# One core, two layers: the first norm's factor and offset folded into the second modulation's rows in two partitions

## The chip, the cores and the metric

The kernel runs on one core of a Trainium2 chip. Its time is device time in microseconds (us), from the start of the program to its end. The kernel before took 1130.2 us, the median of three runs (1126.81, 1130.2 and 1132.19).

The core has five engines with instruction queues of their own: TensorE (PE in the profile; PEld is its weight loads), VectorE (DVE), ScalarE (ACT), GpSimd (POOL) and SyncE (SP), which here only issues transfers (DMAs). Each engine works its queue in order, and waits on semaphores for the others.

## The reference, cut to what matters

One step of a network of two layers for 128 context tokens and 256 latent tokens, with 1024 columns. Each layer has a token mixer and a mixture of experts (MoE). Both are modulated by six rows that come from a conditioning vector, one set for the latent tokens and one for the context tokens:

```python
m = silu(cvec) @ w_ada + b_ada                     # 6 x 1024 columns
sh1, sc1, g1, sh2, sc2, g2 = split(m, 6)
mix = token_mixer(x * (1 + sc1) + sh1)
x = layer_norm(ALPHA * x + g1 * mix, ln1_g, ln1_b)
y = hier_moe(x * (1 + sc2) + sh2)
x = layer_norm(ALPHA * x + g2 * y, ln2_g, ln2_b)
```

What the MoE reads is therefore, with n the normed row before its factor and offset, `(n * ln1_g + ln1_b) * (1 + sc2) + sh2`. This equals `n * G + B`, with `G = ln1_g * (1 + sc2)` and `B = ln1_b * (1 + sc2) + sh2`. G and B are two rows of 1024 numbers for each of the two token sets. Both kernels work with G and B; they differ in where these are formed.

## The kernel before, in words

**Tiles.** The 384 tokens are three tiles of 128 partitions (tile 0 the context, tiles 1 and 2 the latents). Weights stream from HBM through a ring of buffers `w_raw` of 1 MB; ScalarE and VectorE split each piece into two parts (`wr`, lines 102 and 110), and TensorE multiplies it as three products (lines 97 to 99 and 488 to 490).

**The modulation rows.** The generator `ada(l, g)` works out a third of the six rows of layer l: g = 0 gives sh1 and sc1, g = 1 gives g1 and sh2, g = 2 gives sc2 and g2. TensorE's result lies in four stretches of 512 columns, and stretch t in the two partitions 32t and 32t + 1 (latent and context row). That is the tile `adasb`. For g = 1 and 2 the bias row is added to it (line 243), for g = 2 the first two stretches get + 1 (line 245), and four small transfers on GpSimd's queue write it into a table in DRAM, `m_d` (line 247). The generator runs beside the mixer: the loop `mixer` calls it again every few weight pieces, and the instructions between two `yield`s come in one go.

**After the mixer.** `open_ln1` frees the mixer's tiles and loads rows from `m_d`, each spread over all 128 partitions: g1 (line 891), sc2 and sh2, and the norm's factor `lg` and offset `lb`. On GpSimd it then forms G in the place of sc2 and B in the place of sh2: three passes over 128 x 1024 for each token set, six for a layer (lines 911 to 913, product `rtmp` first). Meanwhile TensorE runs the output projection (lines 488 to 490), column block by column block. For each tile of a block VectorE multiplies the result by g1 (line 946, which reads PSUM), adds ALPHA x (line 949, both inputs in SBUF) and takes the norm's statistics (line 952); TensorE transposes the sum for the router (line 963) and multiplies it (line 970). The last block stands in `last_col`: there VectorE applies G (line 999) and B (line 1002) to the whole row, and the routing follows, then the MoE.

**What sets the order.** In the mixer a scheduler places the instructions on each engine: it simulates the program with a cost model and takes what is ready first. The first 50 us (`start`, the table STEPS) and `last_col` stand in an order written by hand. SyncE's transfers stand in one queue. In the built program each of them waits, besides for its buffer, for an earlier transfer: there are eight semaphores taken in turn (DMAHW0 to 7), and a transfer waits until the one before it on its semaphore has landed.

Of the kernel before, what the change touches and what calls it, by code (L numbers as in the profile page):

```python
# [20 lines left out]
D = 1024  # L21
# [58 lines left out]
class Kern:  # L80
# [130 lines left out]
    def ada(self, l, g):  # L211

        nc, a = self.nc, self.a
        ps = self.bank("ms")
        for kp in range(4):
            for k in range(2):
                w = self.get(("a", l, g, kp, k))
                for t in range(4):
                    nc.tensor.matmul(ps[32 * t:32 * t + 32, :], self.cT[:, 2 * kp + k, :],  # L219
                                     w[:, t * 512:t * 512 + 512],  # L220
                                     start=(kp == 0 and k == 0), stop=(kp == 3 and k == 1))
                self.done()
            yield
        sb = self.mix.tile([128, 512], F32, tag="tmp", name="adasb", bufs=3)
        self.act(sb, ps, AF.Copy)
        yield
        p2 = self.bank("ms")
        for j in range(4):
            nc.tensor.transpose(p2[:, j * 128:(j + 1) * 128], sb[:, j * 128:(j + 1) * 128], self.ident)
        mT = self.mT[l]  # L230
        nc.vector.tensor_tensor(
            mT[:, g * 16:(g + 1) * 16, :].rearrange("p (t j) s -> p j t s", j=4),
            p2.rearrange("p (j t r) -> p j t r", j=4, t=4)[:, :, :, 0:2],
            self.bT[:, l, g * 16:(g + 1) * 16].rearrange("p (t j) -> p j t", j=4)
            .unsqueeze(3).to_broadcast([128, 4, 4, 2]),
            op=ALU.add)
        if g != 1:
            j = 8 if g == 0 else 32
            nc.vector.tensor_scalar(mT[:, j:j + 8, :], mT[:, j:j + 8, :], 1.0, None, op0=ALU.add)
        if g > 0:  # L240
            br = self.mix.tile([128, 512], F32, tag="tmp", name="adabr", bufs=3)
            nc.sync.dma_start(br, a["badar"][l * 2 + g - 1])
            nc.vector.tensor_tensor(sb, sb, br, op=ALU.add)
            if g == 2:
                nc.vector.tensor_scalar(sb[0:64, :], sb[0:64, :], 1.0, None, op0=ALU.add)
            for t in range(4):
                nc.gpsimd.dma_start(self.m_d[l][g - 1, :, t * 512:(t + 1) * 512], sb[32 * t:32 * t + 2, :])
        yield
# [627 lines left out]
    def open_ln1(self, l):  # L876
# [12 lines left out]
        def load(name, src, pool):  # L889
            t = pool.tile([128, 1024], F32, tag=name if pool is self.lp else "row", name=name, bufs=1 if pool is self.lp else 2)  # L890
            nc.sync.dma_start(t, src.to_broadcast([128, 1024]))
            rows[name] = t
            return t
# [6 lines left out]
        src = a["x"] if l == 0 else self.x_d  # L900
        nc.sync.dma_start(xs[0], src[0:256, :].rearrange("(i p) c -> p i c", p=128))
        nc.sync.dma_start(xs[1][:, 0], src[256:T, :])
        g = load("lg", a["ln"][l * 4:l * 4 + 1, :], self.mo)
        b = load("lb", a["ln"][l * 4 + 1:l * 4 + 2, :], self.mo)
        for s in range(2):
            load(f"sc2{s}", md[1, s:s + 1, 0:1024], self.lp)
            load(f"sh2{s}", md[0, s:s + 1, 1024:2048], self.lp)
        for s in range(2):
            sc, sh = rows[f"sc2{s}"], rows[f"sh2{s}"]
            t = self.lp.tile([128, D], F32, tag="t", name="rtmp", bufs=2)  # L910
            nc.gpsimd.tensor_tensor(t, sc, b, op=ALU.mult)  # L911
            nc.gpsimd.tensor_tensor(sh, sh, t, op=ALU.add)
            nc.gpsimd.tensor_tensor(sc, sc, g, op=ALU.mult)
        self.st1 = self.sm.tile([128, NT, 4, 6], F32, tag="st1", name="st1", bufs=1)

    def route_consts(self, l):
# [1056 lines left out]
```

## Time and profile before

| what | value |
|---|---|
| runs | 1126.81, 1130.2, 1132.19 us; median 1130.2 |
| profiled execution: own time, span of the trace | 1127.33 us, 1125.6 us |
| TensorE busy, share of the span | 1011.2 us, 90% |
| VectorE busy | 810.7 us, 72% |
| ScalarE busy | 417.4 us, 37% |
| GpSimd busy | 269.7 us, 24% |
| mean granted clock of TensorE | 0.959 of full speed |

A busy share is a mean over stages with different limits. Layer 0's mixer ends near 372 us and its MoE near 555 us; layer 1's mixer runs from some 590 to 918 us, and its MoE to the end. In the listings a time is us from the span's start, and the bracket at a row's end is the engine's idle time before that instruction and what ended it.

### The profile page before, as it was taken

How to read it: one execution, taken by the hardware profiler on the slowest of the kernel's cores; microseconds unless marked ns; L12 is line 12 of the kernel's file. 1: busy time of each engine (PE TensorE's matmuls, PEld its weight loads, DVE VectorE, ACT ScalarE, POOL GpSimd, SP SyncE). 2: the span in 40 equal slices, each digit the busy share in tenths (PEclk: the TensorE clock that was granted, in tenths of full speed). 3: DMA queues.
4: the chain of work that ended last, by engine and by line, in shares of the span. 5: the costliest groups of instructions: out<-in, count | busy, mean ns of one | idle time of the engine just before them, and what ended most of it. 6: DMA issues, size and time to landing. Idle time of an engine off the chain costs nothing. (4 is left out here: it accounts for less than half of the span.)

```text
span 1125.6 us, 20806 instructions
## 1 busy us (share of the span) xinstructions
PE 1011.2 (90%) x8182; PEld 840.7 (75%) x8182; DVE 810.7 (72%) x1530; ACT 417.4 (37%) x753; POOL 269.7 (24%) x232
## 2 busy tenths in 40 slices
PE   7999999999999999776689998999999999778673
PEld 5898978877999988433259897788999998754322
DVE  4399999965446986762569999997834587777437
ACT  4324254434333324341163443445532341434221
POOL 0001431221100510333244043114111025013335
PEclk9999999999999989897989999999999999989888
DMA  9967668447436667799585756773223666689955
GB/s 358 412 241 257 266 217 294 178 163 270 151 112 246 259 262 293 303 420 403 219 315 201 280 217 233 251 290 127 110 94 132 224 244 229 227 317 416 419 204 194
DMA packets 55101, 282.75 MB, mean 251 GB/s; under 512 B 8060, under 2 KB 12284, under 8 KB 27857
## 3 DMA queue, kind: packets, MB, share of 16 engines
q1 hardware_dynamic: 49632, 270.01, 63.1%
q0 software_dynamic: 5360, 11.29, 2.7%
q8 instruction: 69, 1.13, 0.4%
q14 instruction: 40, 0.32, 0.1%
HBM read 262.13 MB, written 24.71 MB: 255 GB/s over the span
## 5 line engine op out<-in xcount | busy, mean ns | idle before, releaser
L97 PE MATMUL ps_mm<-hThi,wr 128*128 128x384 f32 x672 | 229.9, 343 | 4.4 <-ACT hThi L102 2.3
L110 DVE TENSOR_TENSOR wr<-w_raw,wr 128x1024 fp32r<-128x1024 f32 x124 | 162.2, 1309 | 92.4 <-ACT wr L102 92.3
L98 PE MATMUL ps_mm<-hTlo,wr 128*128 128x384 f32 x672 | 228.0, 340 | 0.6 <-DVE hTlo L441 0.4
L99 PE MATMUL ps_mm<-hThi,wr 128*128 128x384 f32 x672 | 227.5, 339 | 0.6 <-DVE wr L110 0.6
L102 ACT ACTIVATE wr<-w_raw 128x1024 fp32r<-128x1024 f32 x140 | 147.5, 1055 | 68.1 <-PE ps_mm L99 37.8
L505 DVE SCALAR_TENSOR_TENSOR cacc<-pad,par,cacc 128x399 f32<-128x399 f32 x240 | 169.2, 705 | 4.2
L97 PEld LDWEIGHTS ps_mm<-hThi,wr 128*128 128x128 f32 x672 | 127.1, 189 | 18.2 <-issue 4.0
L98 PEld LDWEIGHTS ps_mm<-hTlo,wr 128*128 128x128 f32 x672 | 127.1, 189 | 6.3 <-DVE hTlo L441 2.5
L99 PEld LDWEIGHTS ps_mm<-hThi,wr 128*128 128x128 f32 x672 | 127.2, 189 | 2.5 <-DVE wr L110 0.9
L110 POOL TENSOR_TENSOR wr<-w_raw,wr 128x1024 fp32r<-128x1024 f32 x10 | 24.5, 2447 | 201.6 <-ACT wr L102 201.2
L1458 POOL DMA_INDIRECT y_d<-ys,dst x28 | 28.4, 1016 | 172.3 <-DVE hv L1400 73.3
L1446 PE MATMUL ps_sc<-w,hidT 128*32 128x512 f32 x256 | 43.1, 766 | 28.6 <-ACT ys L102 21.9
L1415 PE MATMUL ps_mm<-hv,win 128*32 128x128 f32 x1024 | 46.4, 277 | 9.2 <-DVE hv L1400 7.8
L1400 DVE COPY hv<-w_raw 128x512 f32 x60 | 41.9, 737 | 16.6 <-PE ps_mm L1415 10.8
L1415 PEld LDWEIGHTS ps_mm<-hv,win 128*32 128x32 f32 x1024 | 35.8, 112 | 22.7 <-DVE hv L1400 12.0
L1409 PE MATMUL ps_mm<-w_raw,win 128*32 128x256 f32 x640 | 47.8, 391 | 3.5 <-ACT win L102 3.5
L219 PE MATMUL ps_ms<-w_raw,cT 128*32 128x512 f32 x320 | 48.7, 612 | 1.4 <-DMA w_raw<-in_wada 1.4
L102 ACT ACTIVATE gate<-ps_mm 128x384 f32<-128x384 f32 x40 | 19.6, 490 | 81.6 <-PE ps_mm L99 80.5
L1446 PEld LDWEIGHTS ps_sc<-w,hidT 128*32 128x32 f32 x256 | 8.2, 123 | 45.8 <-ACT ys L102 32.9
L911 POOL TENSOR_TENSOR rtmp<-sc,lb 128x1024 f32<-128x1024 f32 x4 | 9.8, 2478 | 121.8 <-DMA lb<-in_ln 121.8
L842 POOL TENSOR_TENSOR merged<-merged,gate 128x384 f32<-128x384 f32 x16 | 18.1, 1135 | 87.0 <-DVE gate L841 87.0
L102 ACT ACTIVATE win<-xT 128x256 f32 x64 | 21.5, 409 | 37.6 <-PE ps_mm L1409 30.2
(505 smaller groups left out, 2355.7 us busy)
## 6 DMA issues: line engine op xcount, KB each, us to landing
w_raw<-in_wst SPq DMA_DIRECT2D x68, 1024.0 KB, 6.4
w_raw<-in_wada SPq DMA_DIRECT2D x48, 1024.0 KB, 5.4
w_raw<-in_w SPq DMA_DIRECT2D x40, 1024.0 KB, 10.7
w<-in_w SPq DMA_DIRECT2D x32, 1024.0 KB, 12.3
w_x<-in_w SPq DMA_DIRECT2D x24, 1024.0 KB, 11.8
bias<-in_bias SPq DMA_DIRECT2D x8, 768.0 KB, 7.6
y_d<-zero SPq DMA_DIRECT2D x2, 3072.0 KB, 15.1
yy<-y_d SPq DMA_DIRECT2D x6, 1024.0 KB, 7.1
```

Source lines behind the costliest of these rows:

```text
L97: mm(out, whi, xhi, start=first, stop=False)
L98: mm(out, whi, xlo, start=False, stop=False)
L99: mm(out, wlo, xhi, start=False, stop=last)
L102: return self.nc.scalar.activation(out, in_, f, **k)
L110: (eng or self.nc.vector).tensor_tensor(lo, x, hi.bitcast(F32), op=ALU.subtract)
L219: nc.tensor.matmul(ps[32 * t:32 * t + 32, :], self.cT[:, 2 * kp + k, :], w[:, t * 512:t * 512 + 512], start=(kp == 0 and k == 0), stop=(kp ...
L505: nc.vector.scalar_tensor_tensor(acc, pad[:, j:j + W], w, acc, op0=ALU.mult, op1=ALU.add)
L1400: nc.vector.tensor_copy(hv[:, i, :], src)
L1409: nc.tensor.matmul(ps[e * 32:(e + 1) * 32, 0:256], x[:, k, e * 32:(e + 1) * 32], w[:, e, kk, :], start=k == 0, stop=k == 7, skip_group_che ...
L1415: nc.tensor.matmul(ps[t * 32:(t + 1) * 32, 256:384], x[:, k, 128 + i * 32:160 + i * 32], hv[:, i, kk, h * 128:(h + 1) * 128], start=False, ...
L1446: nc.tensor.matmul(po[e * 32:(e + 1) * 32, :], hT[:, e * 32:(e + 1) * 32], w2[:, e, :], start=True, stop=True)
L1458: ins = nc.gpsimd.indirect_dma_start(out=view, out_offset=bass.IndirectOffsetOnAxis(ap=dst, axis=0), in_=rows, in_offset=None, bounds_chec ...
```

## The change

The six passes of `open_ln1` are left out. In their place `ada(l, 2)` forms G and B on VectorE while the rows lie in two partitions per stretch: for the two stretches of sc2 it loads ln1_g, ln1_b (spread over two partitions) and sh2 (from `m_d`, where g = 1 has put it) into three small tiles `lnr`, makes three passes of 2 x 512 for each stretch, and writes B over sh2 in `m_d`; G goes out in place of sc2 with the transfers that were there. There are two more `yield`s in the generator. `open_ln1` still loads `lg` and `lb`. The diff:

```diff
             if g == 2:
+
+                yield
                 nc.vector.tensor_scalar(sb[0:64, :], sb[0:64, :], 1.0, None, op0=ALU.add)
+                lg, lb, sh = (self.mix.tile([64, 512], F32, tag="lnr", name="lnr", bufs=3) for _ in range(3))
+                for t in range(2):
+                    c = slice(t * 512, (t + 1) * 512)
+                    r = slice(32 * t, 32 * t + 2)
+                    for k, x in enumerate((lg, lb)):
+                        nc.sync.dma_start(x[r, :], a["ln"][l * 4 + k:l * 4 + k + 1, c].to_broadcast([2, 512]))
+                    nc.sync.dma_start(sh[r, :], self.m_d[l][0, :, 1024 + t * 512:1024 + (t + 1) * 512])
+                yield
+                for t in range(2):
+                    r = slice(32 * t, 32 * t + 2)
+                    nc.vector.tensor_tensor(lb[r, :], lb[r, :], sb[r, :], op=ALU.mult)
+                    nc.vector.tensor_tensor(lb[r, :], lb[r, :], sh[r, :], op=ALU.add)
+                    nc.vector.tensor_tensor(sb[r, :], sb[r, :], lg[r, :], op=ALU.mult)
+                    nc.gpsimd.dma_start(self.m_d[l][0, :, 1024 + t * 512:1024 + (t + 1) * 512], lb[r, :])
...
-        g = load("lg", a["ln"][l * 4:l * 4 + 1, :], self.mo)
-        b = load("lb", a["ln"][l * 4 + 1:l * 4 + 2, :], self.mo)
+        load("lg", a["ln"][l * 4:l * 4 + 1, :], self.mo)
+        load("lb", a["ln"][l * 4 + 1:l * 4 + 2, :], self.mo)
...
-        for s in range(2):
-            sc, sh = rows[f"sc2{s}"], rows[f"sh2{s}"]
-            t = self.lp.tile([128, D], F32, tag="t", name="rtmp", bufs=2)
-            nc.gpsimd.tensor_tensor(t, sc, b, op=ALU.mult)
-            nc.gpsimd.tensor_tensor(sh, sh, t, op=ALU.add)
-            nc.gpsimd.tensor_tensor(sc, sc, g, op=ALU.mult)
```

Because the scheduler places the mixer's instructions, the change moves others too. On GpSimd, at the end of layer 0's mixer, this stood before (`merged` is the mixer's last GpSimd work, `rs` the norm's):

```order
L842 TENSOR_TENSOR merged<-merged,gate 128x384 x8
L911 TENSOR_TENSOR rtmp<-sc_3492,lb 128x1024
L911 TENSOR_TENSOR rtmp<-sc_3496,lb 128x1024
L912 TENSOR_TENSOR sh_3494<-sh_3494,rtmp 128x1024
L913 TENSOR_TENSOR sc_3492<-sc_3492,lg 128x1024
L912 TENSOR_TENSOR sh_3498<-sh_3498,rtmp 128x1024
L913 TENSOR_TENSOR sc_3496<-sc_3496,lg 128x1024
L117 TENSOR_SCALAR rs<-mv_3877 128x1
L118 TENSOR_TENSOR rs_3878<-rs,mhalf 128x1
```

In the change the norm's two operations follow on `merged`, and four small writes to `m_d` (two of them new) stand earlier, between a split of a weight piece and `ctot`, the sum over the convolution's channels. The change's rows of GpSimd from there on:

```order
L110 TENSOR_TENSOR wr<-w_raw,wr 128x1024
L261 DMA m_d_111<-lnr 2x512
L263 DMA m_d_111<-adasb 2x512
L261 DMA m_d_111<-lnr 2x512
L263 DMA m_d_111<-adasb 2x512
L533 TENSOR_TENSOR ctot<-pad 128x384
L535 TENSOR_TENSOR ctot<-ctot,pad 128x384 x2
```

The six passes are gone from the queue. On VectorE in layer 0, from the first scaling of the attention's rows (`s`) to the gated product `merged`, this stood before (`cacc` is the convolution, `qkh` the split queries and keys, `pad` the convolution's result):

```order
L666 TENSOR_SCALAR s_2003<-s_2003,se 128x384 x2
L505 SCALAR_TENSOR_TENSOR cacc<-pad,par,cacc 128x399
L110 TENSOR_TENSOR qkh<-q,qkh 128x256
L258 TENSOR_TENSOR rf<-rf,mT_106 128x16
L110 TENSOR_TENSOR qkh<-k,qkh 128x384
L505 SCALAR_TENSOR_TENSOR cacc<-pad,par,cacc 128x399
L664 RECIPROCAL se<-se 128x2
L509 TENSOR_SCALAR pad<-cacc,par 128x128
L510 TENSOR_SCALAR pad<-cacc,par 128x256
L666 TENSOR_SCALAR s_2058<-s_2058,se 128x384 x2
L110 TENSOR_TENSOR wr<-w_raw,wr 128x1024
L839 SCALAR_TENSOR_TENSOR merged<-gate,ps_mm 128x384
```

In the change the six new passes stand in the same stretch; the split `wr` and `merged` come right behind the last row:

```order
L258 TENSOR_TENSOR lnr<-lnr,adasb 2x512 x2
L682 TENSOR_SCALAR s_2003<-s_2003,se 128x384 x2
L521 SCALAR_TENSOR_TENSOR cacc<-pad,par,cacc 128x399
L110 TENSOR_TENSOR qkh<-q,qkh 128x256
L274 TENSOR_TENSOR rf<-rf,mT_106 128x16
L110 TENSOR_TENSOR qkh<-k,qkh 128x384
L259 TENSOR_TENSOR lnr<-lnr 2x512
L260 TENSOR_TENSOR adasb<-adasb,lnr 2x512
L259 TENSOR_TENSOR lnr<-lnr 2x512
L680 RECIPROCAL se<-se 128x2
L260 TENSOR_TENSOR adasb<-adasb,lnr 2x512
L521 SCALAR_TENSOR_TENSOR cacc<-pad,par,cacc 128x399
```

Six passes came in ahead of `merged`, and the two `pad` rows and the scaling of `s_2058` went behind it. On SyncE, within the first loads of layer 0, four loads of `lnr` came in among the big ones. The change's rows of that stretch (before, it was the same list without the `lnr` rows, the pieces of `in_wada` next to each other):

```order
L826 DMA k<-in_ctxk 128x128
L629 DMA cv<-in_ctxv 128x128
L253 DMA lnr<-in_ln 2x512
L314 DMA w_raw<-in_wst 128x1024 x2
L314 DMA x_77<-in_x 128x3x256
L314 DMA w_raw<-in_wada 128x2048
L253 DMA lnr<-in_ln 2x512 x3
L314 DMA w_raw<-in_wada 128x2048
L314 DMA x_77<-in_x 128x3x256
L314 DMA w_raw<-in_wada 128x2048 x2
```

So the second of the two pieces of `in_wada` waits, in the turn of eight semaphores, for the first `lnr` load, where it had waited for a load of `k` before.

## Rows read from the trace of the kernel before

**Rows 1.** Busy tenths in 40 slices of the span, two engines, the page's part 2.
```profile
PE   7999999999999999776689998999999999778673
DVE  4399999965446986762569999997834587777437
```
**Rows 2.** The chain of waits, in order of time: start, us, what (one row).
```profile
1043.42 22.22 DMA w<-in_w
```
**Rows 3.** By line: count, min/median/max ns, first and last start, form (GpSimd's passes).
```profile
L911 POOL TENSOR_TENSOR rtmp<-sc,lb x4: 2394/2476/2567, 376.0 to 924.8; 128x1024 f32<-128x1024 f32 x4
...
L913 POOL TENSOR_TENSOR sc<-sc,lg x4: 2575/2584/3355, 383.4 to 935.7; 128x1024 f32<-128x1024 f32 x4
```
**Rows 4.** VectorE beside them: three rows in time, then two lines' groups.
```profile
376.40 2.30 DVE L949 SCALAR_TENSOR_TENSOR r<-xs,r 128x256 f32<-128x256 f32 x1
...
379.29 0.40 DVE L946 TENSOR_TENSOR r<-ps_sc,g 128x256 f32<-128x256 f32 x1
...
384.13 2.96 DVE L110 TENSOR_TENSOR wr<-w_raw,wr 128x1024 fp32r<-128x1024 f32 x1
...
L949 DVE SCALAR_TENSOR_TENSOR r<-xs,r x24: 405/426/2301, 373.9 to 952.6; 128x256 f32<-128x256 f32 x24
...
L110 DVE TENSOR_TENSOR wr<-w_raw,wr x124: 1205/1220/3024, 51.6 to 928.3; 128x1024 fp32r<-128x1024 f32 x124
```
**Rows 5.** TensorE in time, where it waited for VectorE's line 949.
```profile
383.81 0.44 PE L963 MATMUL ps_tp<-con,r 128*128 128x128 f32 x2 [0.76 <-DVE r L949]
...
389.65 0.44 PE L963 MATMUL ps_mm<-con,r 128*128 128x128 f32 x2 [1.30 <-DVE r L949]
...
933.58 0.44 PE L963 MATMUL ps_mm<-con,r 128*128 128x128 f32 x2 [0.71 <-DVE r L949]
```
**Rows 6.** SyncE's issues in time around the output projection, layer 0 and layer 1.
```profile
371.66 2.70 SPq L332 DMA_DIRECT2D w_raw<-in_w  x2
...
406.05 3.42 SPq L332 DMA_DIRECT2D w_x<-in_w  x4
...
917.12 2.70 SPq L332 DMA_DIRECT2D w_raw<-in_w  x2
...
949.98 3.43 SPq L332 DMA_DIRECT2D w_x<-in_w  x4
```
**Rows 7.** Layer 0 where the new passes go: VectorE, GpSimd, TensorE, and line 243's group.
```profile
224.90 0.29 DVE L509 TENSOR_SCALAR pad<-cacc,par 128x128 f32<-128x128 f32 x1
225.10 0.35 DVE L510 TENSOR_SCALAR pad<-cacc,par 128x256 f32<-128x256 f32 x1
225.36 1.36 DVE L666 TENSOR_SCALAR s<-s,se 128x384 f32<-128x384 f32 x2
226.64 1.89 DVE L110 TENSOR_TENSOR wr<-w_raw,wr 128x1024 fp32r<-128x1024 f32 x1
...
219.94 2.40 POOL L110 TENSOR_TENSOR wr<-w_raw,wr 128x1024 fp32r<-128x1024 f32 x1 [0.36 <-issue]
...
229.05 0.44 PE L97 MATMUL ps_mm<-hThi,wr 128*128 128x384 f32 x1 [1.51 <-DVE merged L839]
...
L243 DVE TENSOR_TENSOR adasb<-adasb,adabr x4: 675/677/681, 121.5 to 769.4; 128x512 f32<-128x512 f32 x4
```
**Rows 8.** Layer 1 at the same place: VectorE in time.
```profile
767.52 1.02 DVE L660 TENSOR_TENSOR s<-ps_sc,bias 128x384 f32<-128x384 f32 x2 [2.22 <-PE ps_sc L99]
```
**Rows 9.** The first loads: SyncE's issues and TensorE in time.
```profile
18.22 1.33 SPq L298 DMA_DIRECT2D w_raw<-in_wst  x2
...
21.89 0.92 SPq L298 DMA_DIRECT2D w_raw<-in_wada  x2
...
32.70 0.33 SPq L298 DMA_DIRECT2D rope<-in_rope  x1
...
32.07 1.96 PE L193 MATMUL ps_ms<-w_raw,cT 128*32 128x128 f32 x64
```
**Rows 10.** SyncE in layer 0 where the reads of m_d come in.
```profile
124.48 3.62 SPq L332 DMA_DIRECT2D w_raw<-in_wada  x2
```

## The prediction

> **What bounds the kernel now.** I read the busy tenths first [rows 1]. With 28.1 us to a slice, TensorE's row stands at 9 from slice 1 to 15 and, but for one 8, from 21 to 33; these hold both mixers and their output projections, so there TensorE is the bound, and VectorE is the next: it is at 9 in slices 2 to 7, during layer 0's convolution, and again in slices 21 to 26. From slice 34 on TensorE falls to 8 and less, and the chain of waits at the end runs over transfers, such as 22.22 us for one piece of the experts' weights [rows 2]. Those transfers are issued when earlier buffers come free, so what starts earlier there ends earlier; a saved microsecond must come from TensorE's idle time ahead of the MoE.
>
> The six passes that the change removes are 2.5 us each [rows 3]. They run in the output projection: the first starts at 376.0 us in layer 0, the last at 935.7 in layer 1. Nobody waits for them: G and B are first read in `last_col`, and in the list of waits there no engine stands behind lines 911 to 913. So their own time, twelve passes or 30 us over both layers, is worth nothing by itself. What they do cost is VectorE's time beside them: line 949 takes 2.30 us at 376.40 against a median of 0.426, and the split of a weight piece 2.96 us at 384.13 against 1.220 [rows 4]. The third question is whether TensorE feels this, and the answer is three stalls on line 949: 0.76 and 1.30 us in layer 0, 0.71 in layer 1 [rows 5].
>
> **The rule on the shared port.** Line 946, between the two long ones, reads one input from PSUM and keeps its 0.40 us [rows 4]; line 949 and the split read both from SBUF and stretch. The Trainium skill says the same ("SBUF — State Buffer", section "Who interferes with whom"): a VectorE instruction with two SBUF inputs contends with a GpSimd instruction that reads SBUF, and the later one is blocked until the other has finished. The trace agrees: the excess of 1.9 and 1.7 us is below one GpSimd pass of 2.5. The rule also speaks against this change, since the new passes have two SBUF inputs: where a GpSimd pass runs, each could be held for the rest of it, and by that the added term of part 2 would grow by up to one GpSimd split, 2.40 us [rows 7].
>
> **Part 1: the passes leave the projection.** The gain is TensorE's stalls there: 0.76 + 1.30 + 0.71 = 2.77 us [rows 5]. Between them TensorE is busy without a gap, so a faster VectorE finds nothing more to give. That a stall here does move the MoE I read from the two layers: from the issue at the projection's start to the issue of `w_x` it is 34.39 us in layer 0 (371.66 to 406.05) and 32.86 in layer 1 (917.12 to 949.98) [rows 6]. The difference of 1.53 us is about the 1.35 by which layer 0's stalls are longer. So I take −2.77 whole. What is late next is TensorE itself.
>
> **Part 2: six passes of VectorE in layer 0.** The trace has no pass of 2 x 512; the nearest row is line 243, 128 x 512 in 0.677 us [rows 7], and I take it for partitions worked side by side. Six are 4.1 us; as successive starts on VectorE lie some 0.08 us closer than the durations, 3.6 us of its queue. They stand ahead of `merged`, and there TensorE did wait, 1.51 us until 229.05 [rows 7]. Ahead of `merged` the change takes away the two `pad` rows and the scaling of `s_2058`: from 224.90 to the split's start at 226.64 that is 1.74 us [rows 7], and +3.6 − 1.74 = +1.86. The split right before `merged` took 1.89 us against its median of 1.22 [rows 4, 7]; of that I give back 0.66, since `ctot`, which ran beside it on GpSimd and waits for `pad`, now starts later. That leaves +1.2 us of stall. The bounds: −1.5, if the new order lifts the present stall altogether, and +4.1, if nothing of what moved helps. I take +1.2, the value from the rows of this very place.
>
> **Part 3: the same in layer 1.** VectorE has idle time there: it waits 2.22 us for TensorE just before 767.52 [rows 8], and the page shows VectorE at 7 and 8 tenths in slices 27 and 28, 760 to 816 us, while TensorE stands at 9 [rows 1]. Six passes add 3.6 us between the modulation and `merged`; I cost them at 0.5 us, hidden behind TensorE's queued products, and with that cover gone at 4.1. It is not below nothing, since the rows show no stall of TensorE to lift at this place.
>
> **Part 4: transfers.** Per layer SyncE issues six more, of 4 KB each. In the first 50 us of layer 0 four of them stand among loads that keep the transfers busy, and the second piece of `in_wada` now waits for the first `lnr`, which goes out just ahead of 18.22 [rows 9]. Its issue, the second in the row at 21.89, slips by some 2.5 us. The piece must be there at 33.05, half way through the 64 products that start at 32.07; by the issue at 32.70, which waits for it on the same semaphore, it had landed at 32.70 [rows 9]. So its slack is 0.35 us. Yet between it and 18.22 stand two half pieces, a quarter of x and a whole piece, some 2.4 MB, so a later issue need not land later: I cost it at 0, at most 2.5 − 0.35 = 2.2. The reads of sh2 from `m_d` stand between the two issues at 124.48 [rows 10] and hold the second until the writes have landed, a microsecond or so; the next pieces are for products several us on, so 0, at most 1.5. GpSimd's two more writes per layer stand ahead of `ctot`, for which the convolution's chain waits; its result is used by the third branch alone, two dozen weight pieces later: 0.
>
> **The sum.** −2.77 + 1.2 + 0.5 = −1.1 us. On the profiled execution's own time that is 1127.33 − 1.1 = 1126.2. This execution lies 2.9 us under the median of the runs, 1130.2, and within their spread; a median is compared with a median, so the predicted time is 1130.2 − 1.1 = 1129.1, say 1129 us. A change of 0.5%, 5.7 us, is about what a measurement can tell from none here.
>
> **Rivals.**
> *VectorE's new passes become TensorE's stall.* In both layers nothing that moved makes room, and the passes stand on the path at full length: 4.1 + 4.1 = 8.2, less 2.77, is +5.4, hence 1135.6; with GpSimd's split [rows 7] over them once a layer, 4.8 more, 1140.4. For it: VectorE at 9 tenths up to slice 7, 225 us, and the stall at 229.05. Against: VectorE drops to 6 in slice 8 and has gaps in layer 1. It decides from the point where the new stalls in the two mixers pass 2.77 us together.
> *The new order is a better one.* The scheduler has placed some hundred mixer instructions anew. If the stall at 229.05 goes as well and the new passes are hidden, it is −2.77 − 1.51 = −4.3; hence 1125.9; with TensorE's other short waits in the mixers partly gone too I put it as low as −7, 1123. For it: `pad`, which the new order puts behind `merged`, was not urgent. Against: no work of TensorE goes away.
> *The gain is swallowed.* The MoE waits for its transfers anyway, so the 2.77 us stop there, and the added 1.7 counts: 1131.9. For it: the long transfers of the chain [rows 2]. Against: the two layers' difference in [rows 6].
> *The change doesn't do what it says.* If the stretch of line 949 came from the loads that run at the same time and not from GpSimd, the stalls would stay, with the same price as the swallowed gain. Line 946's 0.40 in between speaks against it; I count it there.
>
> **How the numbers follow.** Forecast 0.48, with its own range 1126 to 1132; swallowed or unchanged 0.14; better order 0.21, of it 0.16 past −5.7 us, since some hundred moved instructions have no bound that rows can show; new stalls 0.17, of which 0.13 past +5.7. So faster 0.16, slower 0.13, the same 0.71. The range for 8 in 10 takes in the edges of both sides: 1123 to 1136.
>
> **What would show it.** In the new profile lines 911 to 913 are gone; the maximum of line 949 falls from 2.30 to near 0.45 and that of the split next to the projection to near 1.23; TensorE's three stalls vanish, and from the projection's start to `w_x` it is some 32 us in both layers. The new lines 258 to 260 take some 0.68 us each. The first `merged` behind them shows a stall of TensorE of 2 to 3 us in layer 0, and none over 1 us in layer 1. In the first 50 us TensorE's products with `in_wada` start by 32.1 without a wait for a transfer. I am wrong if the stalls of line 949 stay, if the MoE starts earlier and ends no earlier, or if the mixers' stalls change by more than 4 us in sum.

## The result: slower by 1.1%

The change takes 1143.26 us, the median of five runs (1138.28 to 1144.99), where the kernel before takes 1130.2; the ratio of the runs is 1.0106, its 95% interval 1.0069 to 1.0143. Two further measurements of the same two kernels gave 1.012 (1.009 to 1.015) and 1.0114 (1.0082 to 1.0146). The forecast was 1129 us with a range of 1123 to 1136: the time lies 14 us above the forecast and outside the range.

The profiled execution of the change took 1143.26 us, with a span of 1141.5, 15.9 more than before. I cut both spans at the same points of the program: from 128 us (up to there both stand within 0.1 us of each other) to the first product of the output projection, to the last one, to the first product of line 99 in the next layer (a few of that layer's products stand ahead of it), and so on for layer 1. Each row is one stretch: its length, then the busy time of TensorE, its weight loads, VectorE, ScalarE and GpSimd, the granted clock of TensorE (1.00 is 2.4 GHz, 0.50 is 1.2), the DMA share and GB/s. First the kernel before:

```profile
128.00:359.98 231.98, 227.03 (x1363) 200.42 (x1355) 170.11 (x301) 93.22 (x174) 42.88 (x40) 0.99 0.59 215
359.98:407.54 47.56, 45.50 (x374) 45.10 (x373) 39.12 (x62) 13.15 (x22) 18.26 (x10) 1.00 0.59 214
...
578.88:905.45 326.57, 321.97 (x1964) 290.69 (x1964) 254.31 (x411) 131.90 (x230) 76.71 (x67) 0.99 0.54 196
905.45:951.48 46.03, 45.32 (x373) 45.04 (x373) 36.55 (x62) 13.15 (x22) 18.28 (x10) 1.00 0.61 221
```

And the change:

```profile
128.00:368.94 240.94, 234.86 (x1362) 204.12 (x1355) 172.16 (x307) 93.13 (x174) 43.98 (x42) 0.98 0.57 207
368.94:413.96 45.02, 45.02 (x374) 45.01 (x374) 31.03 (x62) 13.17 (x22) 2.36 (x4) 1.00 0.61 224
...
585.73:921.62 335.89, 325.97 (x1964) 293.26 (x1964) 261.56 (x418) 132.46 (x230) 79.04 (x69) 0.98 0.52 191
921.62:966.64 45.02, 45.02 (x373) 45.01 (x373) 31.02 (x62) 13.16 (x22) 2.35 (x4) 1.00 0.62 225
```

The two projections (second and fourth row of each) are 2.54 and 1.01 us shorter, and TensorE has no idle time left in them. The two mixers (first and third) are 8.96 and 9.32 us longer. The experts' stages, left out here, are 0.4 and 0.7 longer. So what was to be gained was gained, and the mixers gave back five times as much.

**The projection.** Line 949 of before [rows 4] is 959 here; its group by line in the change:

```profile
L959 DVE SCALAR_TENSOR_TENSOR r<-xs,r x24: 406/425/427, 382.9 to 967.8; 128x256 f32<-128x256 f32 x24
```

SyncE's issues in time, to be set beside [rows 6]:

```profile
380.63 2.70 SPq L348 DMA_DIRECT2D w_raw<-in_w  x2
...
412.47 3.43 SPq L348 DMA_DIRECT2D w_x<-in_w  x4
...
933.30 2.70 SPq L348 DMA_DIRECT2D w_raw<-in_w  x2
...
965.15 3.43 SPq L348 DMA_DIRECT2D w_x<-in_w  x4
```

The longest of the 24 passes now takes 0.427 us (before 2.301), and from the projection's start to `w_x` it is 31.84 and 31.85 us.

**Layer 0's mixer.** TensorE in time in the change, where [rows 7] has its wait (start, us, instruction; in the bracket the idle time ahead and who ended it):

```profile
230.88 0.69 PE L97 MATMUL ps_mm<-hThi,wr 128*128 128x384 f32 x1 [3.38 <-DVE merged L855]
231.37 0.52 PE L98 MATMUL ps_mm<-hTlo,wr 128*128 128x384 f32 x1
231.69 0.52 PE L99 MATMUL ps_mm<-hThi,wr 128*128 128x384 f32 x1
...
237.12 0.34 PE L98 MATMUL ps_mm<-hTlo,wr 128*128 128x384 f32 x1
237.29 0.34 PE L99 MATMUL ps_mm<-hThi,wr 128*128 128x384 f32 x1
```

VectorE in time, the first of the new passes and `merged`:

```profile
220.46 3.08 DVE L258 TENSOR_TENSOR lnr<-lnr,adasb 2x512 f32<-2x512 f32 x2
...
230.28 0.55 DVE L855 SCALAR_TENSOR_TENSOR merged<-gate,ps_mm 128x384 f32<-128x384 f32 x1
```

The stretch behind the wait by itself, columns as in the stages:

```profile
230.80:237.10 6.30, 6.22 (x19) 6.22 (x20) 3.14 (x9) 0.00 (x0) 3.66 (x3) 0.50 0.32 107
```

TensorE waits 3.38 us for `merged` where it waited 1.51. And then comes what no row of before showed at this place: the granted clock stands at 0.50, so 1.2 GHz, for 6.3 us. Successive products start 0.32 us apart (231.37, 231.69), behind 237.1 they start 0.17 apart again (237.12, 237.29). The 19 products that start from 230.88 on, before 237.12, would take some 3.4 us at full clock (0.28 for the first, as in the kernel before, 0.17 for each of the others): another 2.8 us are lost, more than the 1.87 by which the stall grew.

The third part of layer 0's loss is no idle time at all. The modulation's products (line 219, four stretches of columns) come in blocks of 16 (counted in the trace's records, of which each product of the source has two). TensorE in time in the kernel before:

```profile
246.19 1.92 PE L219 MATMUL ps_ms<-w_raw,cT 128*32 128x512 f32 x16
...
285.10 1.06 PE L219 MATMUL ps_ms<-w_raw,cT 128*32 128x512 f32 x8
```

And in the change:

```profile
256.02 1.05 PE L219 MATMUL ps_ms<-w_raw,cT 128*32 128x512 f32 x2
257.71 1.92 PE L219 MATMUL ps_ms<-w_raw,cT 128*32 128x512 f32 x14
```

The scheduler, which places some hundred instructions anew around the passes, has cut three blocks in two here. Two products alone hold TensorE as long as eight, and the fourteen left take as long as sixteen. In the groups by line, from 190 to 300 us, the same 80 products take 10.9 us before and 14.0 in the change. These times count the end of each piece, which overlaps with what follows; from the start of each piece to the start of what follows it, the difference is 2.9 us.

Of the 8.96 us of layer 0's mixer, 1.13 are idle time (6.08 in place of 4.95, by the stage rows), 2.8 the clock and 2.9 the cuts; 2.1 I can't assign.

**Layer 1's mixer.** VectorE in time in the change:

```profile
783.24 1.40 DVE L274 TENSOR_TENSOR rf<-rf,mT 128x16 f32<-128x16 f32 x1
...
789.01 1.78 DVE L260 TENSOR_TENSOR adasb<-adasb,lnr 2x512 f32<-2x512 f32 x1
...
791.42 1.49 DVE L110 TENSOR_TENSOR qkh<-q,qkh 128x256 fp32r<-128x256 f32 x1
792.83 1.34 DVE L110 TENSOR_TENSOR qkh<-k,qkh 128x384 fp32r<-128x384 f32 x1
794.10 0.54 DVE L855 SCALAR_TENSOR_TENSOR merged<-gate,ps_mm 128x384 f32<-128x384 f32 x1
```

GpSimd in the same time:

```profile
781.87 2.74 POOL L110 TENSOR_TENSOR wr<-w_raw,wr 128x1024 fp32r<-128x1024 f32 x1 [3.44 <-ACT wr L102]
...
789.20 1.03 POOL L533 TENSOR_TENSOR ctot<-csq 128x384 f32<-128x384 f32 x1
...
791.61 2.15 POOL L535 TENSOR_TENSOR ctot<-ctot,csq 128x384 f32<-128x384 f32 x2
```

TensorE's two waits there:

```profile
789.12 0.44 PE L97 MATMUL ps_mm<-gmhi,wr 128*128 128x384 f32 x1 [1.03 <-ACT gate L102]
...
794.69 0.69 PE L97 MATMUL ps_mm<-hThi,wr 128*128 128x384 f32 x1 [3.19 <-DVE merged L855]
```

And the stretch behind the second:

```profile
794.60:800.30 5.70, 5.61 (x18) 5.61 (x18) 3.43 (x6) 0.00 (x0) 0.00 (x0) 0.50 0.18 47
```

In the kernel before VectorE itself waited for TensorE ahead of this `merged`; its row there:

```profile
781.23 0.56 DVE L839 SCALAR_TENSOR_TENSOR merged<-gate,ps_mm 128x384 f32<-128x384 f32 x1 [0.67 <-PE ps_mm L99]
```

In the change TensorE waits for it, 3.19 us, with 1.03 ahead of that, and the clock falls again: 5.7 us at 0.50, which by the spacing of the products lose 2.6 us. The passes do more than their own 4.1 us. Four instructions with two SBUF inputs, one of them a pass, are held while GpSimd reads: `rf` 1.40 in place of 0.16, the pass 1.78 in place of 0.67, the two `qkh` 1.49 and 1.34 in place of the 0.42 and 0.56 that they take in layer 0. Together 4.2 us. Of the 9.32 us, 5.3 are idle time (9.92 in place of 4.60) and 2.6 the clock; 1.4 are left. Cuts explain none of it: layer 1's modulation products take 1.0 us less than before.

### The profile page after: what moved, and what is told of

The parts are those of the page before. It is cut to its first block, busy times and chain, and to the rows that moved or that the text cites. A ratio compares the mean times of both kernels' runs of the same rounds, so it can differ in the third digit from the quotient of the medians.

```text
span 1141.5 us, 20844 instructions
## 1 busy us (share of the span) xinstructions
PE 1024.7 (90%) x8182; PEld 851.6 (75%) x8182; DVE 804.1 (70%) x1542; ACT 417.4 (37%) x753; POOL 242.7 (21%) x224
## 3 DMA queue, kind: packets, MB, share of 16 engines
q8 instruction: 69, 1.13, 0.4%
## 5 line engine op out<-in xcount | busy, mean ns | idle before, releaser
L97 PE MATMUL ps_mm<-hThi,wr 128*128 128x384 f32 x672 | 233.0, 347 | 9.8 <-DVE merged L855 6.6
L110 DVE TENSOR_TENSOR wr<-w_raw,wr 128x1024 fp32r<-128x1024 f32 x124 | 159.9, 1290 | 106.9 <-ACT wr L102 106.7
L99 PE MATMUL ps_mm<-hThi,wr 128*128 128x384 f32 x672 | 229.5, 342 | 1.2 <-DVE wr L110 1.2
L97 PEld LDWEIGHTS ps_mm<-hThi,wr 128*128 128x128 f32 x672 | 128.9, 192 | 24.5 <-DVE merged L855 8.3
L99 PEld LDWEIGHTS ps_mm<-hThi,wr 128*128 128x128 f32 x672 | 128.9, 192 | 4.0 <-issue 1.8
L1425 PE MATMUL ps_mm<-hv,win 128*32 128x128 f32 x1024 | 49.4, 280 | 10.0 <-DVE hv L1410 8.5
L1425 PEld LDWEIGHTS ps_mm<-hv,win 128*32 128x32 f32 x1024 | 38.8, 114 | 23.2 <-DVE hv L1410 12.5
L1419 PE MATMUL ps_mm<-w_raw,win 128*32 128x256 f32 x640 | 50.2, 400 | 3.1 <-ACT win L102 3.1
L1419 PEld LDWEIGHTS ps_mm<-w_raw,win 128*32 128x32 f32 x640 | 26.5, 115 | 12.2 <-ACT win L102 4.1
```

Source lines behind the costliest of these rows:

```text
L97: mm(out, whi, xhi, start=first, stop=False)
L99: mm(out, wlo, xhi, start=False, stop=last)
L110: (eng or self.nc.vector).tensor_tensor(lo, x, hi.bitcast(F32), op=ALU.subtract)
L1419: nc.tensor.matmul(ps[e * 32:(e + 1) * 32, 0:256], x[:, k, e * 32:(e + 1) * 32], w[:, e, kk, :], start=k == 0, stop=k == 7, skip_group_che ...
L1425: nc.tensor.matmul(ps[t * 32:(t + 1) * 32, 256:384], x[:, k, 128 + i * 32:160 + i * 32], hv[:, i, kk, h * 128:(h + 1) * 128], start=False, ...
```

## The experiments

The kernel before, run beside these versions, lies at 1127.5 to 1129.9 us; each time is to be set beside the one given with it.

### The same passes, elsewhere: late_passes and held_back

In both, `ada` is as in the kernel before, and the passes stand in the mixer, behind one more trip of the rows through DRAM. The first places them by the number of the weight piece:

```diff
+            if n == 48:
+                self.late_loads(l)      # ln1_g, ln1_b, sh2 and sc2 into four lnr tiles
+            if n == 52:
+                self.late_passes(l)     # the same six passes, and four writes to m_d
```

> The same six passes on VectorE, but formed in the mixer some 15 weight pieces later, where VectorE is busy 4 to 5 tenths, from the rows as they lie in the table in DRAM (two more small reads per layer); the generator of the modulation rows is as in the kernel before, without the two extra yields. Theory A: no new stall at `merged`, granted clock at 1.00 through both mixers behind their start, the gain of the output projection (2.8 us) stays: 1126 to 1130 us. Rival B (the scheduler's other order costs, wherever the passes stand): blocks of the modulation's products on TensorE are cut in more pieces, about 1 us for each cut: 1130 to 1135 us. Rival C (the added transfers cost): 1138 us or more.

Measured: 1130.87 us beside 1127.47, ratio 1.0018 (0.9997 to 1.0038). Neither theory's number separates here. The rows tell why: the scheduler had pulled the passes forward, since they were ready, in layer 1 to where the change has them. VectorE in time there, the first two:

```profile
781.06 1.39 DVE L267 TENSOR_TENSOR lnr<-lnr 2x512 f32<-2x512 f32 x2
```

A stall of 2.63 us followed, on VectorE's scaling of the attention's rows. In layer 0 they ran at 227 to 235 us, three of the six ahead of the first `merged`, and TensorE's wait for it was 1.07 us. So "late in the code" was not late on the engine, and the second version holds them by an order:

```diff
-                        nc.vector.scalar_tensor_tensor(g, g, 1.0, pss[b][:, :T], ...)
+                        gi = nc.vector.scalar_tensor_tensor(g, g, 1.0, pss[b][:, :T], ...)
+                        if br == 1 and d == 1:
+                            with tc.issue_after(gi.ins):
+                                self.late_loads(l)
+                        if br == 1 and d == 3:
+                            with tc.issue_after(gi.ins):
+                                self.late_passes(l)
```

> The same six passes and transfers as in the run with the late passes, but now held by an explicit order behind the gating of the second branch (the scheduler had pulled them forward to the place of the change, 781 to 787 us in layer 1). The order on TensorE and VectorE up to there is the one of the kernel before. Theory A: stall at `merged` in layer 0 as in the kernel before, 1.5 us, none in layer 1, clock at 1.00 behind; both mixers together within 2 us of the kernel before, and the output projection 2.8 to 3.5 us shorter: 1123 to 1127 us beside 1127.5. Rival B (the passes or their transfers cost wherever they stand): 1130 us or more.

Measured: 1124.66 beside 1129.92, ratio 0.9952 (0.9935 to 0.9970): half a per cent faster than the kernel before, and so faster than the change. TensorE's wait at `merged` in layer 0:

```profile
231.35 0.45 PE L97 MATMUL ps_mm<-hThi,wr 128*128 128x384 f32 x1 [1.51 <-DVE merged L862]
```

One of the passes in layer 0 on VectorE:

```profile
294.77 0.67 DVE L268 TENSOR_TENSOR lnr<-lnr 2x512 f32<-2x512 f32 x1
```

Its mixers and its first projection, cut and with columns as the stages above:

```profile
128.00:362.43 234.43, 228.94 (x1367) 201.28 (x1359) 174.88 (x308) 93.83 (x174) 45.65 (x44) 0.99 0.58 214
362.43:407.44 45.01, 45.01 (x373) 45.00 (x373) 31.02 (x62) 13.16 (x22) 2.36 (x4) 1.00 0.61 224
...
580.11:906.69 326.58, 321.93 (x1963) 290.63 (x1963) 258.36 (x417) 131.91 (x230) 79.29 (x71) 0.99 0.54 196
```

The stall is again 1.51, the blocks are whole, layer 1's mixer is 326.58 (before 326.57), and the projections keep their gain (the second is 45.02 too). Layer 0's mixer is 2.45 us longer than before, but that has arisen by 165 us, ahead of the passes: half a microsecond is there at the first modulation product already, and most of the rest comes near 150 us, where the clock stays low for longer. First this version, then the kernel before:

```profile
149.70:156.60 6.90, 6.55 (x27) 4.26 (x29) 6.87 (x17) 2.24 (x5) 2.20 (x4) 0.51 0.47 160
...
148.50:155.40 6.90, 6.90 (x39) 4.20 (x37) 6.87 (x15) 3.13 (x6) 2.19 (x3) 0.76 0.58 193
```

From the modulation product that follows (at 162.48 us before, at 164.78 here) to the projection the two differ by 0.15 us. So the same six passes, with their loads and writes, cost nothing that these rows can tell at 291 to 297 and 836 to 842 us. What cost was the place. This traced execution (1128.17 us) is one of the slower of its ten and no faster than that of the kernel before; that the version is faster rests on the medians.

### Half of VectorE's time at the same place: three_passes

```diff
-                nc.vector.tensor_scalar(sb[0:64, :], sb[0:64, :], 1.0, None, op0=ALU.add)
...
-                for t in range(2):          # three passes of 2 x 512, twice
+                v = sb[0:64, :]
+                nc.vector.scalar_tensor_tensor(lb, v, 1.0, lb, op0=ALU.add, op1=ALU.mult)
+                nc.vector.tensor_tensor(lb, lb, sh, op=ALU.add)
+                nc.vector.scalar_tensor_tensor(v, v, 1.0, lg, op0=ALU.add, op1=ALU.mult)
```

> The change with three passes over 64 partitions in place of six over two partitions (both stretches in one pass), the addition of 1 taken into two of them; same place, same two extra yields, the small tiles loaded over all 64 partitions. VectorE's own time for it falls from some 4.1 us + 0.4 to some 2 us per layer. Theory A (VectorE's time ahead of `merged`, past a stall of some 3 us with the clock on top): the stalls at `merged` fall to 2 us or less in both layers, the granted clock stays at 1.00 behind them, and the time is 1130 to 1136 us. Rival B (the new order, the transfers or the buffers held longer, not VectorE's time): 1140 to 1146 us.

Measured: 1131.17 beside 1127.47, ratio 1.0030 (1.0009 to 1.0050), as theory A has it. The yields are those of the change, and the loads are as many, each spread over 32 partitions; the addition of 1 goes into two of the passes. Layer 0's `merged` makes TensorE wait no longer, layer 1's 1.19 us, by TensorE's row in time:

```profile
788.00 0.44 PE L97 MATMUL ps_mm<-hThi,wr 128*128 128x384 f32 x1 [1.19 <-DVE merged L855]
```

With the shorter wait the clock behind it stays at 1.00; of the change's 1.1% some 0.8 points are gone with half of VectorE's time. Layer 0's blocks are cut here as often as in the change, and its mixer, from the first modulation product on, is 312.36 us all the same (before 312.09), with no wait at `merged` and no stretch at half the clock to pay for. Layer 1's is still 4.2 us longer; there `rf` is held by GpSimd's split:

```profile
779.42 2.68 DVE L274 TENSOR_TENSOR rf<-rf,mT 128x16 f32<-128x16 f32 x1
```

### VectorE's time alone: six_idle_passes

```diff
                 nc.vector.tensor_scalar(sb[0:64, :], sb[0:64, :], 1.0, None, op0=ALU.add)
+                e, f = (self.mix.tile([64, 512], F32, tag="lnr", ...) for _ in range(2))   # zeroed on GpSimd
+                for t in range(2):
+                    r = slice(32 * t, 32 * t + 2)
+                    nc.vector.tensor_tensor(e[r, :], e[r, :], sb[r, :], op=ALU.mult)
+                    nc.vector.tensor_tensor(e[r, :], e[r, :], f[r, :], op=ALU.add)
+                    nc.vector.tensor_tensor(f[r, :], sb[r, :], f[r, :], op=ALU.mult)
```

> The kernel before, its six GpSimd passes kept, with six more VectorE passes of 2 x 512 per layer at the place where the change has its own (they read the modulation's tile and write scratch tiles that nobody reads); no added loads, no added writes, no added yields. Theory A (VectorE's time ahead of `merged`, with the scheduler's reaction to it, is the whole loss of the mixers): a stall of TensorE at `merged` near 3 us in layer 0 and the granted clock at 0.50 behind it, blocks of the modulation's products cut in more pieces, the two mixers together 10 us or more longer than in the kernel before; 1137 to 1145 us beside 1127.5. Rival B (the four small loads, the reads of m_d, the two more writes or the longer hold of the buffers cost): the mixers at most 3 us longer, 1127 to 1131 us.

Measured: 1143.98 beside 1129.92, ratio 1.0124 (1.0099 to 1.0148): the kernel before becomes as slow as the change by six passes that nobody reads. The change's loads, writes and yields are not needed for it. The parts differ, though: this version's mixers lose 11.8 us and the change's 18.3, of which the projections gave 3.55 back. And how it loses is not what I expected in layer 0. TensorE's wait at `merged`:

```profile
232.19 0.44 PE L97 MATMUL ps_mm<-hThi,wr 128*128 128x384 f32 x1 [1.93 <-DVE merged L847]
```

The stretch behind it:

```profile
232.20:238.50 6.30, 6.30 (x37) 6.26 (x38) 4.96 (x11) 1.79 (x3) 3.38 (x3) 1.00 0.09 17
```

One of the pieces of the modulation's products:

```profile
258.27 1.05 PE L219 MATMUL ps_ms<-w_raw,cT 128*32 128x512 f32 x4
```

The wait is 1.93 us (the scheduler put two of the six passes behind the first `merged`) and the clock stays at 1.00, yet layer 0's mixer is 7.8 us longer (319.93 in place of 312.09, from the first modulation product). The blocks of 16 are cut in two, three and four, and the 80 products take 16.3 us in place of 10.9, by the starts of what follows 5.0 more: 5.0 of the 7.8. So the passes have two ways to cost: they delay VectorE, and with them the scheduler makes an order that is worse on TensorE. Layer 1 loses 3.95 us, through waits of 1.02 and 2.56. (The traced execution, 1139.63 us, is among the two fastest of the six.)

This version keeps GpSimd's six passes, and still its first projection is shorter than that of the kernel before, 45.71 us in place of 47.56:

```profile
369.63:415.34 45.71, 45.32 (x373) 45.03 (x373) 35.92 (x62) 13.16 (x22) 18.38 (x10) 1.00 0.60 221
```

What those passes cost TensorE depends on which of VectorE's instructions they meet: 2.06 us of idle time in that stage before, 0.39 here.

### The wait filled with products: is it the clock?

Behind the two products that `merged` waits for, small ones into a free corner of their PSUM bank:

```diff
                 pss = self.mm_ws(w, 4, 2, *self.cur)
+                if n == 36:
+                    wv = w[0].rearrange("p (k c) -> p k c", k=4)
+                    for i in range(40):      # 24 in keep_warm24
+                        nc.tensor.matmul(pss[1][:, T:512], wv[:, 3, 128:256], self.cur[0][:, 3, 0:128], ...)
```

> The change as it is, with 40 extra small products of TensorE (128 x 128, their result is read by nobody) right behind the two products that `merged` waits for, in each layer; they fill the place where TensorE idles 3.38 us in layer 0 and 3.19 us in layer 1. VectorE's work stays. Theory A (the longer stall at `merged` lets TensorE's granted clock fall to 1.2 GHz, and that costs as much again as the stall): TensorE idles under 1.5 us there, the granted clock stays at 1.00 in the 10 us behind it in both layers, and of 1143.3 us some 3.4 us per layer come back: 1136 to 1138 us. Rival B (the time lies in the stall itself and in the new order of TensorE's work, the clock is no cause): `merged` comes as late as before, so 1142 to 1145 us.

Measured: 1138.78 beside 1127.47, ratio 1.0106 (1.0077 to 1.0136). The clock stayed at 1.00 behind `merged` in both layers, and the mixers were 5.6 us shorter than the change's, but against the kernel before the ratio is that of the change. Forty products took 4.58 us, more than the wait. The repeat on one chip with the change:

> The change with 40 small products in TensorE's wait at `merged`, once more, now beside the change on one chip (the first run of it had only the kernel before beside it and kept the ratio of 1.011). Theory A (the granted clock falls after a stall of 3 us and that costs 3.4 us per layer): 4 to 7 us under the change, the granted clock at 1.00 behind `merged` in both layers. Rival B (the clock there is not what the time depends on, the stage of the experts takes it back or the order costs): within 3 us of the change.

Measured: 1149.34 us. It tells nothing on the clock: this kernel has 18 products of 384 columns in another bank, which stand behind the convolution, and the wait stayed at 3.39 us. The change beside it:

> The change itself once more, beside the next three kernels on one chip, so that their times can be set against it and not only against the kernel before. Both theories: 1.0 to 1.4% above the kernel before.

Measured: 1143.14 beside 1128.16. Then the two once more:

> The change with 24 small products (128 x 128, read by nobody) in TensorE's wait at `merged` in each layer. In the first run of this kind 40 of them took 4.58 us, longer than the wait of 3.4 us that they were to fill; in the second run of that name the products were 18 larger ones in another bank, which the scheduler placed behind the convolution and not in the wait, so it told nothing. By the first run's 0.11 us each, 24 take 2.7 us and end before `merged` comes. Theory A (the granted clock falls after the stall and costs 1.7 to 3.4 us per layer): TensorE idles under 1 us at that place, the granted clock stays at 1.00 in the 10 us behind it in layer 0 and layer 1, `merged` itself comes as late as in the change, and the kernel is 3 to 7 us faster than the change on the same chip. Rival B: the mixers do not get shorter by more than 2 us, since what is lost is the stall and the order.

> The change itself, on the same chip and in the same rounds as the kernel with the 24 small products, for the comparison of the two. Theory A: 3 to 7 us above that kernel. Rival B: within 2 us of it.

Measured: 1140.62 with the products, 1142.11 the change, 1128.8 before. In layer 0 the 24 products fill the wait; in layer 1 `merged` came later in the order built for it, and 3.22 us were left. TensorE in time in that kernel:

```profile
228.20 2.79 PE L854 MATMUL ps_mm<-gmhi,wr 128*128 128x128 f32 x24
231.75 0.44 PE L97 MATMUL ps_mm<-hThi,wr 128*128 128x384 f32 x1 [0.76 <-DVE merged L859]
...
796.30 0.69 PE L97 MATMUL ps_mm<-hThi,wr 128*128 128x384 f32 x1 [3.22 <-DVE merged L859]
```

The stretches behind the two places:

```profile
231.70:238.00 6.30, 6.25 (x38) 6.22 (x39) 3.54 (x8) 2.40 (x5) 3.61 (x3) 1.00 0.27 78
...
796.30:802.00 5.70, 5.70 (x22) 5.60 (x22) 2.60 (x6) 0.07 (x1) 0.00 (x0) 0.54 0.36 111
```

So within one execution: filled, the clock stays; 3.2 us idle, it falls. But the fall is not certain. Of three profiles of the change, all with a wait of 3.38 or 3.39 us in layer 0, one shows 6.3 us at 0.50 behind it, one 3.3 us, one none (1.00). The second and the third:

```profile
230.10:233.40 3.30, 3.24 (x10) 3.24 (x11) 3.12 (x9) 0.00 (x0) 1.23 (x1) 0.50 0.00 0
...
233.70:240.00 6.30, 6.29 (x38) 6.24 (x39) 3.06 (x8) 2.00 (x4) 3.66 (x3) 1.00 0.32 109
```

In layer 1, where two waits of 1.03 and 3.2 us stand close together, all three show 0.50 for 5.7 us or more. Nor is the length of one wait all that counts: the stretch at half the clock near 150 us in the kernel before stands behind a wait of 1.78 us. The 1.5 us between the two medians is within their scatter, so the clock's price as a part of the kernel's time stays open; what stands is the price in the rows, 2.6 to 2.8 us each time it falls for some 6 us.

### Whole blocks: whole_blocks and held_whole

```diff
-            for k in range(2):
-                w = self.get(("a", l, g, kp, k))
+            ws = [self.get(("a", l, g, kp, k)) for k in range(2)]
+            with self.tc.tile_critical():
+                for k in range(2):
```

> The change with the products of the modulation bound together: the scheduler must place all products of one step as one block (in the traces so far a block that is cut in two takes 0.98 us longer, 2.83 in place of 1.85 us; the change has three more cuts than the kernel before in layer 0, the kernel before has cuts in layer 1 too). Theory A (order): no cut is left, the modulation's products take 3 us less in layer 0 and some 4 us less in layer 1; the passes of VectorE stay where they are and so the stalls at `merged`, which this order may move: 1133 to 1139 us where the change has 1143. Rival B (cuts are filled with other work and cost nothing): within 3 us of the change.

> The version with the passes held back, with the modulation's products bound together as well. Theory A: the gain of the projection as in that version and, from six cuts fewer in layer 1, some 4 us more: 1119 to 1124 us where the kernel before has some 1129. Rival B (a block that must come whole makes TensorE wait for its weights, or pushes the pieces that VectorE waits for): 1125 us or more.

Measured: 1188.53 and 1174.93 beside 1128.16 (ratios 1.0531 and 1.0413); both far slower: neither theory of the first, rival B of the second. The blocks are whole, but TensorE stops ahead of them, for both of their weight pieces at once and for things the products don't need (`gmt` is one). The list of its waits in the first version, 100 to 420 us (who waits and for whom: us in total, times, longest):

```profile
PE ps_ms L220 <- DMA w_raw<-in_wada: 4.7, 1, 4.7
PE ps_ms L220 <- POOL gmt L617: 2.6, 1, 2.6
```

The cure was worse than the cut, so the price of a cut, 0.98 us, is read from the rows of several kernels and not shown by an experiment of its own.

### G and B from where they are: from_mT and from_mT2

The router's constants need G and B in columns anyway (`rf`, three passes of 128 x 16, 0.16 us each). These versions transpose them on TensorE and write them out:

```diff
+                G, B_ = self.fold_ln(mT[:, 32:40, :], mT[:, 24:32, :], self.lnT[:, l, :], 0, "rf")
+                p3 = self.bank("ms")
+                for z, x in enumerate((G, B_)):
+                    nc.tensor.transpose(p3[0:16, z * 128:(z + 1) * 128], x.rearrange("p j s -> p (j s)"), self.ident)
+                self.act(gb, p3[0:16, 0:256], AF.Copy)
+                for z in range(2):
+                    nc.gpsimd.dma_start(self.gb_d[l][z]..., gb[:, z * 128:(z + 1) * 128])
```

> No pass on VectorE is added and the six of GpSimd are gone: G and B, which the router's constants form in columns anyway (the rows `rf`, 128 x 16), are formed once in the generator, transposed by two small products of TensorE, copied by ScalarE and written to DRAM in two transfers; the loads of sc2 and sh2 after the mixer read that table. Theory A: only the gain of the output projection is left, less some 0.5 us for the two transpositions: 1126 to 1130 us, no stall at `merged` above 2 us, clock 1.00 in the mixers. Rival B (the new order of the scheduler costs by itself): 1131 to 1137 us.

Measured: 1126.64 beside 1127.47, ratio 0.9993 (0.9974 to 1.0012): no difference that can be told, though the time lies where A has it, since the kernel before was faster on this chip. Without the needless addition and writes:

> The version that takes G and B from the router's columns, without what it leaves useless: the addition of 1 to the two stretches of sc2 on VectorE (0.41 us per layer) and the writes of sc2 and sh2 (four small transfers per layer on GpSimd's queue). Theory A: the gain of the projection less the two transpositions, and 0.4 us less at `merged`: 1122 to 1126 us beside 1127.5, 0.5 to 1 us under the version with them. Rival B: no difference to the kernel before, 1127 to 1129 us, since the experts' stage waits for its transfers in any case.

Measured: 1125.23 beside 1129.92, ratio 0.9966 (0.9945 to 0.9986). Faster than the kernel before, and so than the change; its interval overlaps with that of the version that holds the passes back, so neither of the two is shown to be the better one.

## Why the prediction was wrong

**Part 1, the projection (−2.77 us): right.** The stages are 2.54 and 1.01 us shorter, 3.55 in sum. The three stalls are gone, the 32 us to `w_x` came out as 31.84 and 31.85, and the version held back keeps this gain in its projections. The size is less certain than the sign: with GpSimd's passes still there, the first projection of six_idle_passes has 0.39 us of idle time and not 2.06.

**Part 2, layer 0 (+1.2 us): the step that failed is its list of what a longer wait costs.** The stall was forecast to grow by 1.2 us, to 2 to 3, and grew by 1.87, to 3.38; the passes' 0.68 us held but for one at 2.37, beside GpSimd's split (the prediction gave that a bound of 2.40 and left it out of the sum). What was not in the sum is the clock behind the wait (2.8 us in this execution) and the cut blocks (2.9 us); in all the mixer is 8.96 us longer, 2.1 of it unassigned. The prediction costed the moved instructions on VectorE alone. That TensorE's products had been moved too it says, but it put a worse order of them at nothing without a reason: its one word on this, "no work of TensorE goes away", stands against a better order. The rows from 246 to 285 us show that order has a price.

**Part 3, layer 1 (+0.5 us): wrong, 9.3.** The step was "hidden behind TensorE's queued products". The evidence for it was one idle time of VectorE, 2.22 us before 767.52 [rows 8], and a busy share of 7 to 8 tenths. But the passes went not there, but to 781 to 791 us, and there VectorE's slack ahead of `merged` was 0.67 us. GpSimd's split and `ctot` held them and their neighbours by another 4.2 us. The Trainium skill's rule ("SBUF — State Buffer", section "Who interferes with whom"), by which a VectorE instruction with two SBUF inputs contends with a GpSimd instruction that reads SBUF, was in the prediction as a threat to the passes of layer 0, priced at one split; the trace agrees, and shows it on four instructions, one of them a 128 x 16 one at 1.40 us.

**Part 4, transfers (0): right.** TensorE's products with `in_wada` start at 32.02 us (before 32.07), and the six passes without any transfer cost as much as the change.

**The rivals.** "VectorE's new passes become TensorE's stall" is what happened, at +13 in place of +5.4 (with the split +10.2). Its mechanism was right, and its 8.2 us of new stalls are 6.45 in the rows; its price had no clock and no cuts in it. I gave it 0.17, mainly for layer 1's gaps, a mean over a slice where the question was one wait.

**What would show it.** The sign that I named for being wrong, mixers' stalls changed by more than 4 us in sum, came: TensorE's idle time in them went from 9.55 to 16.0 us. In layer 1 the first `merged` made TensorE wait 3.19 us, where the prediction had none over 1.

## What to carry to other kernels

Work that nobody waits for should be put where the engine that takes it has idle time ahead of every instruction that the bound engine waits for; read that from the one wait, not from a busy share, and hold it there by an order, since a scheduler takes it as soon as it is ready. When work is added to a stage whose order a scheduler makes, look at the new order of the bound engine itself, above all at small products that were together and are now apart. A wait of TensorE that grows from 1.5 to over 3 us can cost more than its growth, through the clock behind it; here the clock fell so in two executions of three in layer 0, and in all three in layer 1.

## What the runs showed that I had not expected

- Modulation products (128 x 32 weights, 512 columns) in a piece of 2, 4, 6 or 8 hold TensorE 0.97 to 1.00 us, in a piece of 10, 12, 14 or 16 1.83 to 1.85, from their start to that of what follows. This holds in all profiles but those with bound blocks, save for pieces that stand in a stretch at half the clock. A block of 16 that is cut in two takes 0.98 us more wherever the cut falls, save in the middle. So the time goes with the number of started eights, that is, of rounds over the four stretches of columns. By 0.99 us for eight and 1.85 for sixteen, a round is 0.86 us and a change to these products and back 0.13, both of them estimates from these rows. The Trainium skill ("TensorEngine Tiling (Array Packing)", section "Key Properties") says that a change of tiling mode drains TensorE; it gives no time. By the estimate such a change is the small part of a cut's price, and the round that is opened and not filled the large one; no run tries the two against each other.
- A wait of 3.4 us ahead of the same product left the clock at 1.00 in one execution and brought it to 0.50 for 3.3 and 6.3 us in two others.
- A 128 x 16 pass of VectorE, 0.16 us by itself, took 1.40 us beside a GpSimd instruction, and 2.68 in three_passes.
